# A Strassen output projection in a hybrid encoder block: loads asked for in another order, rows split in halves, stores and row sums placed later

## The chip, the cores and the metric

The kernel runs on one core of one Trainium2 chip. The metric is device time in microseconds (us) of one execution; a version's figure is the median of its runs. The trace counts from the span's start.

## The reference

One encoder block, sequence 1024, width 1024. All operands are float32. A short gated convolution mixer (`ya`) and a bidirectional gated DeltaNet (`yb`) are projected, gated, merged, projected again, added to the input and normalised:

```python
ya = a_cg * dwconv_centred(a_bg * a_x, conv_a_w[l])
ya = ya * jax.nn.silu(a_z)
ya = ya @ w_pa[l]
...
yb = (o * jax.nn.silu(z)).reshape(bsz, slen, VAL_DIM).astype(dt_)
yb = yb @ w_pb[l]
merged = jax.nn.sigmoid(gate_a_raw) * ya + jax.nn.sigmoid(gate_b_raw) * yb
x = x + gate[:, None, :] * (merged @ w_o[l])
return rmsnorm(x, final_norm_w)
```

## The kernel before

Every float32 product is made of three one-pass matmuls: each operand is split into `hi` (a rounded copy, made by ScalarE, ACT) and `lo` (the rest, `raw - hi`, made by VectorE, DVE, or by GpSimd, POOL), and hi·hi, lo·hi and hi·lo are added in PSUM. So before TensorE (PE) can use a row or a weight, three things have come one after another: a load, an ACT copy and a subtraction.

The order of the program, late stages first in importance here:

- **Up to about 765 us**: projections and the DeltaNet, ordered by a scheduler in the code (`Scheduler`).
- **The pairs, 765 to 1109 us** (the loop over `steps`, L1549): column blocks two at a time by Strassen's method, seven products of 12 matmuls each per pair instead of eight. Groups are `bg`, `ax`, `cg`, `az` for four pairs, then gates `gb`. After each `az`, the mixer's output rows `y` are stored (`y_d`), and `y_sum` (L1439) makes the sums `T1`, `T3`, `T2`, `T4` of their quarters, which the next stage's Strassen products take as operands; they are stored to `t_d`. A list `late` holds such DVE jobs; each step of the loop pops one.
- **Gate blocks 6 and 7** (`gate_block`, L1480), plain products, 1109 to 1131 us.
- **Stage pa, the output projection `ya @ w_pa`** (the loop over `pa_steps`, L1598), 28 steps, four Strassen pairs of seven products, 1131 to 1227 us. Its operands are 28 half-row tiles `yop` (`B11`, `B21`, `B22` from `y_d`; `T1` to `T4` from `t_d`), loaded by `fetch_operand` and split by `split` (L1545: ACT, then DVE). The first pair's products are A11, A12, S4, S2, S1, S3, then, after one product of the second pair, A22. S1 needs `T1`, S3 `T3`, A22 `T4`. S3 and A22 add into the PSUM bank of S2, so they also wait until the earlier content has been copied out to `u_pa`. Weights come through `Pair.load` (four raw tiles `wr_pa` per pair), `prep` (the sums `S_pa` on DVE and the hi copy on ACT) and `rest` (the lo part on DVE).
- **Stage pb, `yb @ w_pb` and the merge** (L1645), eight blocks `j` of 48 matmuls, 1227 to 1322 us. Its rows `yb` are fetched by `fetch_b` into the slots of `yop` tiles that pa has finished with, then split into `bhi`, `blo`. Its weights `wpb[j]` go through `wtile`: two raw tiles `wraw` (two buffers, which the rows of `w_o`, `wor`, use as well), ACT for `wh_pb`, POOL for `wl_pb`. Each product is multiplied by `sgb`, added to the loaded row `mr` and split again (`mhi`, `mlo`).
- **The final projection `merged @ w_o`** and the norm, to the end.

From the pairs to the end of pa, DVE, ACT, POOL and SP each run in the order in which the code is written (`manual_schedule`); from pb on, a scheduler in the compiler orders them, and `tc.high_priority()` lets it hoist. PE runs its list in order. All loads and stores of these stages are issued by SyncE (SP), one queue: an entry that waits holds up all behind it. Line numbers in the profile are those of this kernel; L323 is a helper that records every operation of the earlier stages.

Of the kernel before, what the change touches and what calls it, by code (L numbers as in the profile page):

```python
# [9 lines left out]
F32 = mybir.dt.float32  # L10
# [6 lines left out]
P = 128  # L17
# [311 lines left out]
def block(ctx: ExitStack, tc: tile.TileContext, x, c, wada, wadag, badaT, nwT, win, wab, cva, cvq,  # L329
          alog, dtb, gnw, wpa, wpb, wo, fnw, out, dbg=None):  # L330
# [37 lines left out]
    def ch(c, w=P):  # L368
        return slice(w * c, w * c + w)
# [875 lines left out]
    def bank(pl, name):  # L1245
        return pl.tile([P, 512], F32, tag="b", name=name)

    def wtile(src, name):
        hi = wp.tile([P, KT * P], F32R, tag="whi", name=f"wh_{name}")
        lo = wp.tile([P, KT * P], F32R, tag="wlo", name=f"wl_{name}")  # L1250
        for q in range(2):
            raw = wp.tile([P, 512], F32, tag="wraw", name=f"wr_{name}_{q}")
            Q.dma_start(raw, src[:, ch(q, 512)])
            S.activation(hi[:, ch(q, 512)], raw, AF.Copy)  # L1254
            G.tensor_tensor(lo[:, ch(q, 512)], raw, hi[:, ch(q, 512)].bitcast(F32), ALU.subtract)  # L1255
        return hi, lo
# [138 lines left out]
    def mixed(name, j0, place):  # L1395
        seen = [0, 0]

        def full(n, b):
            if (n, b) not in outs:
                outs[n, b] = btile("out", f"{n}{j0 + b}", 4, (P, T))  # L1400
            return outs[n, b]

        def consume(b, half, ps, add):
            sl = ch(half, 512)
            x = xpads[b][:, 2 + 512 * half : 514 + 512 * half]
            seen[b] += 1
# [24 lines left out]
            if seen[b] == 2:
                Q.dma_start(y_d[j0 + b], a)
            if sum(seen) == 4:
                late.extend(partial(y_sum, j0 // 2, i, *[outs.pop((n, b)) for n in ("a", "c") for b in range(2)])
                            for i in range(1))

        return Pair(name, j0, consume, place)

    def y_sum(m, i, a0, a1, c0, c1):  # L1439

        r11, r12, r21, r22 = (t[:, ch(h, 512)] for t in (a0, a1) for h in range(2))
        t1, t3, t2, t4 = (t[:, ch(h, 512)] for t in (c0, c1) for h in range(2))
        V.tensor_tensor(*((t1, r12, r11), (t3, r22, r12), (t2, r22, t1), (t4, r21, t2))[i], ALU.subtract)
        if i % 2:
            Q.dma_start(t_d[m, i // 2], (c0, c1)[i // 2])
        if i < 3:
            late.insert(0, partial(y_sum, m, i + 1, a0, a1, c0, c1))

    def conv3(acc, b, j, i):
        x, c = xpads[b][:, 1 + i : 1 + i + T], cva_t[:, j, i : i + 1]  # L1450
# [40 lines left out]
        steps.pop(0)  # L1491
        pairs[0].after(n, early[n])
    yop = {n: [None] * 4 for n in hop}
    pas = []

    def merged_pair(j0, place):
        gates = []

        def load_gates():
            for b in range(2):  # L1500
                gates.append(btile("out", f"sga{j0 + b}", 4, (P, T)))
                Q.dma_start(gates[b], sga_d[j0 + b])

        seen = [0, 0]

        def consume(b, half, ps, add):
            g = gates[b][:, ch(half, 512)]
            if add is not None:
                t = btile("tmp", f"t_pa{j0}{b}{half}", 2)
                V.tensor_tensor(t, ps, add, ALU.add)  # L1510
# [79 lines left out]
    def fetch_b(k):  # L1590
        for i, l in enumerate((bhi, blo)):
            p, kk = places[2 * k + i]
            l.append(hp.tile([P, T], F32R, tag=f"h{p}{kk}", name=f"b{('hi', 'lo')[i]}{k}", bufs=1))
        Q.dma_start(blo[k].bitcast(F32), yb_d[k])

    todo = [(n, m) for n in ("T1", "T3", "T4") for m in range(4)]
    fetched = {"S3": (2, 3), "S1": (4, 5), "A22": (6, 7)}
    for i, (p, n) in enumerate(pa_steps):  # L1598
        look_ahead(pa_steps, i + AHEAD + 5)
        advance(pa_steps, i + AHEAD)  # L1600
        for _ in range(2):
# [6 lines left out]
        if i == len(pa_steps) - 10:
            for k in range(2):
                fetch_b(k)  # L1610
        if p is pas[-1] and n in fetched:
            for k in fetched[n]:
                fetch_b(k)
        if i >= len(pa_steps) - 6:
            for k in ((0,), (1,), (2, 3), (4,), (5, 6), (7,))[i - len(pa_steps) + 6]:
                split(bhi[k], blo[k])
# [25 lines left out]
    with tc.tile_pool(name="ms", bufs=2, reuse_waits="tile", side="right") as ms:  # L1642
        sc_t = ms.tile([P, T], F32, tag="sc", name="sc_g", bufs=1)
        Q.dma_start(sc_t, sc_d.to_broadcast([P, T]))
        for j in range(8):  # L1645
            with tc.high_priority():
                w = wtile(wpb[j], f"pb{j}")
            m = ms.tile([P, T], F32, tag="m", name=f"mr{j}")
            Q.dma_start(m, m_d[j])
            sg = ms.tile([P, T], F32, tag="sg", name=f"sgb{j}")  # L1650
            Q.dma_start(sg, sgb_d[j])
            wt = ms.tile([P, T], F32, tag="wadag", name=f"wadag{j}")
            Q.dma_start(wt, wadag[j])
            for half in range(2):
                ps = product(w, bhi, blo, half, f"pb{j}")
                sl = ch(half, 512)
                V.tensor_tensor(sg[:, sl], ps, sg[:, sl], ALU.mult)
                G.tensor_tensor(m[:, sl], m[:, sl], sg[:, sl], ALU.add)
# [124 lines left out]
```

## Time and profile before

| | |
|---|---|
| median of 3 runs | 1420.57 us (1417.34 to 1420.83) |
| profiled execution | 1419.85 us |
| its span in the trace | 1418.1 us |
| PE busy in the span | 1362.4 us (96%) |
| DVE, ACT, POOL busy | 919.1, 632.4, 462.8 us |
| mean granted clock of PE | 0.989 |

PE is busy nearly always, so what can be saved is the time in which it stands still or runs at a lower granted clock. A busy share of 100% in a slice says nothing about the rate; the column PEclk does (1.00 is the full clock). "Idle before" an instruction is time in which its engine did nothing, and the arrow names what ended it.

### The profile page before, as it was taken

How to read it: one execution, taken by the hardware profiler on the slowest of the kernel's cores; microseconds unless marked ns; L12 is line 12 of the kernel's file. 1: busy time of each engine (PE TensorE's matmuls, PEld its weight loads, DVE VectorE, ACT ScalarE, POOL GpSimd, SP SyncE). 2: the span in 40 equal slices, each digit the busy share in tenths (PEclk: the TensorE clock that was granted, in tenths of full speed). 3: DMA queues.
4: the chain of work that ended last, by engine and by line, in shares of the span. 5: the costliest groups of instructions: out<-in, count | busy, mean ns of one | idle time of the engine just before them, and what ended most of it. 6: DMA issues, size and time to landing. Idle time of an engine off the chain costs nothing.

```text
span 1418.1 us, 22459 instructions
## 1 busy us (share of the span) xinstructions
PE 1362.4 (96%) x8450; PEld 1135.1 (80%) x8450; DVE 919.1 (65%) x1583; ACT 632.4 (45%) x1535; POOL 462.8 (33%) x702
## 2 busy tenths in 40 slices
PE   5899999999999999999999999999999969899998
PEld 5678888887889888888887878788787848688886
DVE  6868175657667676856766877777676556763335
ACT  5447575664648384745444232223223532423211
POOL 2004837574738474756410000000000100266301
PEclk9999999999999999999999999999999989999999
DMA  9315341515141323323123121121312854586402
GB/s 355 97 60 153 112 92 66 150 38 142 31 119 61 98 82 89 92 60 91 54 97 134 60 99 64 75 89 51 125 49 90 296 178 163 197 302 198 178 15 104
DMA packets 128334, 163.31 MB, mean 115 GB/s; under 512 B 75105, under 2 KB 75489, under 8 KB 128226
## 3 DMA queue, kind: packets, MB, share of 16 engines
q1 hardware_dynamic: 127794, 160.58, 34.9%
q8 instruction: 66, 1.08, 0.3%
q10 hardware_dynamic: 432, 1.31, 0.3%
q14 instruction: 42, 0.34, 0.1%
HBM read 128.16 MB, written 33.69 MB: 114 GB/s over the span
## 4 chain that ended last, share of the span: by engine, by line
PE 85%; DVE 8%; DMA 3%; ACT 2%; issue 2%; POOL 0%; SPq 0%; POOLq 0%; ACTq 0%; DVEq 0%
PE pp_ga L215 6%; PE pp_z L215 6%; PE pp_q L215 6%; PE cb L215 6%; PE pp_v L215 6%; PE pp_k L215 5%; PE ps_cg_S L1348 4%; PE o L215 4%; PE ps_ax_S L1348 4%; PE ps_pa_S L1348 3%; PE ps_az_S L1348 2%; PE pp_pb L1264 2%; PE ps_bg_S L1348 2%; PE fo L1688 2%; PE fo L1687 2%; PE fo L1689 2%
## 5 line engine op out<-in xcount | busy, mean ns | idle before, releaser
L323 POOL TENSOR_TENSOR E<-E,et 128x30 f32<-128x30 f32 (+7 forms) x240 | 122.5, 510 | 16.8
L1255 POOL TENSOR_TENSOR wl_gb<-wr_gb,wh_gb 128x512 fp32r<-128x512 f32 x4 | 5.1, 1294 | 351.5 <-ACT wh_gb L1254 351.5
L323 POOL TENSOR_TENSOR et<-E 128x30 f32<-128x30 f32 (+7 forms) x240 | 109.2, 455 | 30.0 <-DMA E<-s 13.4
L323 DVE SCALAR_TENSOR_TENSOR S<-S,exps,cb 128x128 f32<-128x128 f32 x96 | 29.6, 344 | 59.3 <-PE cb L215 58.5
L1255 POOL TENSOR_TENSOR wl_pb<-wr_pb,wh_pb 128x512 fp32r<-128x512 f32 x16 | 25.1, 1577 | 128.1 <-DMA blo<-yb_d 104.7
L323 ACT ACTIVATE vw<-cb,cols 128x128 f32<-128x128 f32 x112 | 36.3, 364 | 68.1 <-PE cb L215 67.7
L1264 PE MATMUL pp_pb<-blo,wh_pb 128*128 128x512 f32 x128 | 51.5, 402 | 4.2 <-DVE blo L1547 4.2
L215 PE MATMUL pp_z<-hhi,wh_z 128*128 128x512 f32 x128 | 52.8, 412 | 0.0
L215 PE MATMUL pp_z<-hhi,wl_z 128*128 128x512 f32 x128 | 52.7, 412 | 0.0
L215 PE MATMUL pp_z<-hlo,wh_z 128*128 128x512 f32 x128 | 52.7, 412 | 0.0
L215 PE MATMUL pp_ga<-hhi,wl_ga 128*128 128x512 f32 x128 | 51.7, 404 | 0.0
L215 PE MATMUL pp_ga<-hhi,wh_ga 128*128 128x512 f32 x128 | 51.6, 403 | 0.0
L215 PE MATMUL pp_ga<-hlo,wh_ga 128*128 128x512 f32 x128 | 51.5, 402 | 0.0
L323 DVE SCALAR_TENSOR_TENSOR r<-cb,negeg,vp 128x128 f32<-128x128 f32 x112 | 34.5, 345 | 25.4 <-PE cb L215 24.9
L1263 PE MATMUL pp_pb<-bhi,wh_pb 128*128 128x512 f32 x128 | 50.7, 396 | 0.0
L1265 PE MATMUL pp_pb<-bhi,wl_pb 128*128 128x512 f32 x128 | 50.4, 393 | 0.0
L323 ACT ACT_TABLE_LOAD x38 | 48.8, 1283 | 1.5 <-PEq L1778 0.8
L323 DVE SCALAR_TENSOR_TENSOR vT<-xpad,cvq_t,vT 128x1024 f32<-128x1024 f32 x32 | 48.7, 1523 | 0.3
L215 PE MATMUL pp_q<-hhi,wl_q 128*128 128x512 f32 x112 | 44.7, 399 | 2.4 <-issue 2.4
L323 ACT ACTIVATE vn<-cb,cols 128x128 f32<-128x128 f32 x128 | 41.4, 372 | 10.4 <-PE cb L215 10.4
L215 PE MATMUL pp_q<-hhi,wh_q 128*128 128x512 f32 x112 | 45.6, 407 | 0.0
L215 PE MATMUL pp_v<-hhi,wl_v 128*128 128x512 f32 x112 | 45.4, 406 | 0.0
(951 smaller groups left out, 4422.0 us busy)
## 6 DMA issues: line engine op xcount, KB each, us to landing
wada<-in_wada SPq DMA_DIRECT2D x16, 512.0 KB, 8.5
D<-gr_d SPq DMA_DIRECT2D x16, 512.0 KB, 7.1
wr_bg<-in_win SPq DMA_DIRECT2D x18, 256.0 KB, 3.0
xt<-in_x SPq DMA_DIRECT2D x8, 512.0 KB, 8.9
wr_k<-in_win SPq DMA_DIRECT2D x16, 256.0 KB, 2.8
wr_q<-in_win SPq DMA_DIRECT2D x16, 256.0 KB, 2.8
wr_v<-in_win SPq DMA_DIRECT2D x16, 256.0 KB, 3.0
wr_ga<-in_win SPq DMA_DIRECT2D x16, 256.0 KB, 2.9
```

What stands on the lines that cost most here:

```text
L215: getattr(self.pe, what)(out, *ins, **kw)
L323: self._sched.record(self._name, lambda: real(*args, **kw), outs, ins, cost, extra, table, op == "memset", port)
L1255: G.tensor_tensor(lo[:, ch(q, 512)], raw, hi[:, ch(q, 512)].bitcast(F32), ALU.subtract)
L1263: PE.matmul(ps, wh, mhi[k][:, sl], start=i == 0, stop=False)
L1264: PE.matmul(ps, wh, mlo[k][:, sl], start=False, stop=False)
L1265: PE.matmul(ps, wl, mhi[k][:, sl], start=False, stop=i == KT - 1)
L1348: PE.matmul(ps, w, r, start=first and m == i == 0, stop=m == 3 and i == 2, skip_group_check=True)
L1687: PE.matmul(ps, mhi[k][:, ch(t)], wh, start=k == 0, stop=False)
L1688: PE.matmul(ps, mlo[k][:, ch(t)], wh, start=False, stop=False)
L1689: PE.matmul(ps, mhi[k][:, ch(t)], wl, start=False, stop=k == KT - 1)
```

## The change

- **Row sums.** After an `az` pair (the last one excepted), four empty entries go into `late` ahead of the four `y_sum` jobs, so they run four steps later, and on SP their two stores come behind the next four weight loads.
- **Second pair's weights.** `look_ahead(pa_steps, 6)` after gate block 6, so its `wr_pa` loads stand ahead of the loads of `T1`, `T3`, `T4` instead of behind them. The second pair's gate rows `sga`, till now loaded there, are loaded after step 1.
- **Splits of `T1`, `T3`, `T4`** start at step 1 of pa, not 0: two tiles per step.
- **Stores of pa** (`m_d`) are not asked for where the row is complete, but after the next step's product.
- **Rows for pb** are loaded and split in halves of 512 columns; rows 0 and 1 after step 14 (before: 18), split at steps 16 and 17 (before: 22 and 23). Rows 2 to 7 have their first halves split first, the second halves at the last two steps.
- **First weights of pb** are asked for by the code after step 19 and split after step 26, where before the compiler's scheduler had hoisted both (loads at 1112 us).

The diff, without the passing of arguments:

```diff
-                late.extend(partial(y_sum, j0 // 2, i, *[outs.pop((n, b)) for n in ("a", "c") for b in range(2)])
-                            for i in range(1))
+                rows = [outs.pop((n, b)) for n in ("a", "c") for b in range(2)]
+                late.extend([None] * (4 if j0 < 6 else 0) + [partial(y_sum, j0 // 2, i, *rows) for i in range(4)])
...
-                Q.dma_start(m_d[j0 + b], gates[b])
+                stores.append((m_d[j0 + b], gates[b]))
...
-    look_ahead(pa_steps, 7)
-    pas[1].extra()
+    look_ahead(pa_steps, 6)
...
-        Q.dma_start(blo[k].bitcast(F32), yb_d[k])
+        for h in range(2):
+            Q.dma_start(blo[k][:, ch(h, 512)].bitcast(F32), yb_d[k][:, ch(h, 512)])
...
+    last = len(pa_steps)
+    fetched = {last - 14: (0, 1), last - 6: (2, 3), last - 5: (4, 5), last - 4: (6, 7)}
+    split_at = {last - 12: ((0, 0), (0, 1)), last - 11: ((1, 0), (1, 1)), last - 5: ((2, 0), (3, 0)),
+                last - 4: ((4, 0), (5, 0)), last - 3: ((6, 0), (7, 0)), last - 2: ((2, 1), (3, 1)),
+                last - 1: ((4, 1), (5, 1), (6, 1), (7, 1))}
...
-        for _ in range(2):
+        for _ in range(2 * (i > 0)):
...
+        waiting, stores[:] = stores[:], []
         p.product(n)
+        for k in fetched.get(i, ()):
+            fetch_b(k)
+        for dst, src in waiting:
+            Q.dma_start(dst, src)
+        if i in (1, 8, 15):
             pas[i // 7 + 1].extra()
...
+        if i == last - 9:
+            raws = wraws(wpb[0], "pb0")
+        if i == last - 2:
+            w_next = wtile(wpb[0], "pb0", raws)
+        for k, h in split_at.get(i, ()):
+            split(bhi[k][:, ch(h, 512)], blo[k][:, ch(h, 512)])
...
-                w = wtile(wpb[j], f"pb{j}")
+                w = wtile(wpb[j], f"pb{j}") if j else w_next
```

PE's order is the same in both kernels, instruction by instruction. Three places on the other engines follow.

SP, from gate block 6's store (`xpad_119`) to the first load of `T1` (`yop_T_0`), before:

```order
L1485 DMA sgb_d<-xpad_119 128x1024
L1502 DMA sga_10880<-sga_d 128x1024
L1502 DMA sga_10882<-sga_d 128x1024
L1485 DMA sgb_d<-xpad_120 128x1024
L1543 DMA yop_T_0_10976<-t_d 128x512
```

and now:

```order
L1488 DMA sgb_d<-xpad_119 128x1024
L1324 DMA wr_pa_10880<-in_wpa 128x512
L1324 DMA wr_pa_10882<-in_wpa 128x512
L1324 DMA wr_pa_10884<-in_wpa 128x512
L1324 DMA wr_pa_10886<-in_wpa 128x512
L1488 DMA sgb_d<-xpad_120 128x1024
L1546 DMA yop_T_0_10980<-t_d 128x512
```

The second pair's four weight loads stand where the two `sga` loads stood, 1 MB each way; before, they followed all twelve loads of `T1`, `T3` and `T4`.

DVE at the first splits of `T1` (the first `S_pa` rows here are the second pair's weight sums), before:

```order
L1547 TENSOR_TENSOR yop_T_0_10976<-yop_T_0_10976 128x512
L1547 TENSOR_TENSOR yop_T_1_10978<-yop_T_1_10978 128x512
L1310 TENSOR_TENSOR S_pa_11031<-wr_pa_11000,wr_pa_11002 128x512
L1310 TENSOR_TENSOR S_pa_11033<-S_pa_11031,wr_pa_11004 128x512
L1333 TENSOR_TENSOR wloS_pa_10920<-S_pa_11008,whiS_pa_10919 128x512
L1547 TENSOR_TENSOR yop_T_2_10980<-yop_T_2_10980 128x512
L1547 TENSOR_TENSOR yop_T_3_10982<-yop_T_3_10982 128x512
```

and now:

```order
L1315 TENSOR_TENSOR S_pa_11023<-wr_pa_10880,wr_pa_10882 128x512
L1315 TENSOR_TENSOR S_pa_11025<-S_pa_11023,wr_pa_10884 128x512
L1338 TENSOR_TENSOR wloS_pa_10924<-S_pa_11004,whiS_pa_10923 128x512
L1550 TENSOR_TENSOR yop_T_0_10980<-yop_T_0_10980 128x512
L1550 TENSOR_TENSOR yop_T_1_10982<-yop_T_1_10982 128x512
L1513 TENSOR_TENSOR t_pa_11048<-ps_pa_A_11035,e_pa_11021 128x512
L1515 TENSOR_TENSOR sga_10807<-t_pa_11048,sga_10807 128x512
L1338 TENSOR_TENSOR wlS_pa_11028<-S_pa_11025,whS_pa_11027 128x512
L1550 TENSOR_TENSOR yop_T_2_10984<-yop_T_2_10984 128x512
L1550 TENSOR_TENSOR yop_T_3_10986<-yop_T_3_10986 128x512
```

The weight sums now stand ahead of all splits of `T1`, and three other pieces (a PSUM read `t_pa`, its product with `sga`, a weight's lo part) stand between the two halves of `T1`.

ACT in stage pb at block 2's weights (`wh_pb` of `wr_pb_0`, `wr_pb_1`) and block 0's merged rows (`mhi`), before:

```order
L1637 ACTIVATE woh_11824<-wor_1_11822 128x512
L1254 ACTIVATE wh_pb_11828<-wr_pb_0_11830 128x512
L1254 ACTIVATE wh_pb_11828<-wr_pb_1_11834 128x512
L1659 ACTIVATE mhi_11642<-mr_11676 128x512 x2
L1659 ACTIVATE mhi_11643<-mr_11757 128x512
```

and now:

```order
L1649 ACTIVATE woh_11848<-wor_1_11846 128x512
L1259 ACTIVATE wh_pb_11856<-wr_pb_0_11852 128x512
L1671 ACTIVATE mhi_11676<-mr_11700 128x512 x2
L1259 ACTIVATE wh_pb_11856<-wr_pb_1_11853 128x512
L1671 ACTIVATE mhi_11677<-mr_11781 128x512
```

The second half of block 2's weights now stands behind block 0's two merged rows.

More of the change, by code (lines that the diff above doesn't have):

```diff
@@ L1246, in bank, with wraws, wtile @@
         return pl.tile([P, 512], F32, tag="b", name=name)
-    def wtile(src, name):
+    def wraws(src, name):
+        raws = [wp.tile([P, 512], F32, tag="wraw", name=f"wr_{name}_{q}") for q in range(2)]
+        for q, raw in enumerate(raws):
+            Q.dma_start(raw, src[:, ch(q, 512)])
+        return raws
+    def wtile(src, name, raws=None):
+        raws = raws or wraws(src, name)
         hi = wp.tile([P, KT * P], F32R, tag="whi", name=f"wh_{name}")
         lo = wp.tile([P, KT * P], F32R, tag="wlo", name=f"wl_{name}")
-        for q in range(2):
-            raw = wp.tile([P, 512], F32, tag="wraw", name=f"wr_{name}_{q}")
-            Q.dma_start(raw, src[:, ch(q, 512)])
+        for q, raw in enumerate(raws):
             S.activation(hi[:, ch(q, 512)], raw, AF.Copy)
@@ L1445, in y_sum @@
             Q.dma_start(t_d[m, i // 2], (c0, c1)[i // 2])
-        if i < 3:
-            late.insert(0, partial(y_sum, m, i + 1, a0, a1, c0, c1))
     def conv3(acc, b, j, i):
@@ L1493, in block @@
     yop = {n: [None] * 4 for n in hop}
-    pas = []
+    stores = []
     def merged_pair(j0, place):
@@ L1556, in block @@
             p.product(n)
-        if late:
-            late.pop(0)()
+        job = late.pop(0) if late else None
+        if job:
+            job()
         if i + 4 == len(steps):
@@ L1593, in fetch_b @@
             l.append(hp.tile([P, T], F32R, tag=f"h{p}{kk}", name=f"b{('hi', 'lo')[i]}{k}", bufs=1))
-        Q.dma_start(blo[k].bitcast(F32), yb_d[k])
+        for h in range(2):
+            Q.dma_start(blo[k][:, ch(h, 512)].bitcast(F32), yb_d[k][:, ch(h, 512)])
     todo = [(n, m) for n in ("T1", "T3", "T4") for m in range(4)]
-    fetched = {"S3": (2, 3), "S1": (4, 5), "A22": (6, 7)}
+    last = len(pa_steps)
[3 more added lines that the diff above has]
+                last - 1: ((4, 1), (5, 1), (6, 1), (7, 1))}
     for i, (p, n) in enumerate(pa_steps):
@@ L1604, in block @@
                 split(*yop[n4][m])
+        waiting, stores[:] = stores[:], []
         p.product(n)
-        if i in (8, 15):
-            pas[i // 7 + 1].extra()
[L1608 to L1616, printed above, removed]
+        for k in fetched.get(i, ()):
[3 more added lines that the diff above has]
+        if i in (1, 8, 15):
+            pas[i // 7 + 1].extra()
+        if i == last - 9:
[4 more added lines that the diff above has]
+            split(bhi[k][:, ch(h, 512)], blo[k][:, ch(h, 512)])
+    for dst, src in stores:
+        Q.dma_start(dst, src)
     sctx.close()
```

## Prediction

> **What bounds the kernel now.** First the page's busy line: PE is at 96%, so I ask where the other 4% lie, and where PE is busy but slow. The waits of PE, asked for the pairs (690 to 1100 us) and then for stages pa and pb (1080 to 1270 us), give nearly all of it:
>
> ```profile
> PE 1362.4 (96%) x8450; PEld 1135.1 (80%) x8450; DVE 919.1 (65%) x1583; ACT 632.4 (45%) x1535; POOL 462.8 (33%) x702
> ...
> PE ps_bg_S L1348 <- DVE u_bg L1356: 2.5, 4, 0.7
> ...
> PE ps_pa_S L1348 <- ACT yop_T L1546: 8.3, 1, 8.3
> PE ps_pa_S L1348 <- DVE u_pa L1356: 4.7, 1, 4.7
> PE pp_pb L1264 <- DVE blo L1547: 4.2, 3, 3.6
> PE ps_pa_S L1348 <- ACT u_pa L1354: 0.9, 1, 0.9
> ```
>
> The last four add to 18.1 us. The windows show what follows a long wait (second figure PE busy, sixth the granted clock):
>
> ```profile
> 1150.00:1155.00 5.00, 3.23 (x6) 1.77 (x6) 4.29 (x8) 4.46 (x9) 0.00 (x0) 0.50 0.10 37
> 1155.00:1160.00 5.00, 4.14 (x18) 3.40 (x19) 4.90 (x9) 2.37 (x5) 0.00 (x0) 0.98 0.15 52
> 1165.00:1170.00 5.00, 3.58 (x9) 2.83 (x10) 3.86 (x7) 0.91 (x2) 0.00 (x0) 0.55 0.00 2
> ```
>
> After the 8.3 and the 4.7 us waits PE runs at half clock for some microseconds. So I measure each place by PE's own progress. The timeline of PE, where S1 and the second pair's S1 start, then where block 0, 1 and 2 of pb start:
>
> ```profile
> 1141.92 0.63 PE L1348 MATMUL ps_pa_S<-yop_T,whiS_pa 128*128 128x512 f32 x2
> 1174.74 0.63 PE L1348 MATMUL ps_pa_S<-yop_T,whiA_pa 128*128 128x512 f32 x2
> 1227.07 0.40 PE L1263 MATMUL pp_pb<-bhi,wh_pb 128*128 128x512 f32 x1
> 1244.73 0.39 PE L1263 MATMUL pp_pb<-bhi,wh_pb 128*128 128x512 f32 x1
> 1255.72 0.39 PE L1263 MATMUL pp_pb<-bhi,wh_pb 128*128 128x512 f32 x1
> ```
>
> Block 1 takes 10.99 us for 48 matmuls, 0.229 each; block 0 took 17.66, so 6.7 us are lost there. Between the first two rows lie five products, 60 matmuls, 13.7 us at that rate; they took 32.8, so 19.1 us are lost there.
>
> Why S1 waited is read from ACT, DVE and SP:
>
> ```profile
> 1139.33 1.30 ACT L1546 ACTIVATE yop_T<-yop_T 128x512 fp32r<-128x512 f32 x2 [5.12 <-DMA yop_T<-t_d]
> 1150.54 0.63 ACT L1326 ACTIVATE whS_pa<-S_pa 128x512 fp32r<-128x512 f32 x1 [9.42 <-DVE S_pa L1310]
> 1139.99 1.36 DVE L1547 TENSOR_TENSOR yop_T<-yop_T 128x512 fp32r<-128x512 f32 x2 [5.85 <-ACT yop_T L1546]
> 1149.02 0.69 DVE L1310 TENSOR_TENSOR S_pa<-wr_pa,wr_pa 128x512 f32<-128x512 f32 x1 [7.67 <-DMA wr_pa<-in_wpa]
> 1124.88 0.74 SPq L1485 DMA_DIRECT2D sgb_d<-xpad  x1
> 1133.65 0.32 SPq L1485 DMA_DIRECT2D sgb_d<-xpad  x1
> 1134.03 8.19 SPq L1543 DMA_DIRECT2D yop_T<-t_d  x12
> 1142.98 14.16 SPq L1319 DMA_DIRECT2D wr_pa<-in_wpa  x8
> ```
>
> T1's first tiles land at 1139.3 and are split. The other two have to stand behind the second pair's weight sum, whose weights were asked for at 1142.98, behind all twelve T loads, and landed at 1149. It is not the rows that PE waited for, but ACT and DVE held up, in order, by weights that no one needed yet.
>
> **Part 1, the weights and splits in pa.** The four weight loads take the place of two `sga` loads, as many bytes, after gate block 6's store (1124.88). Bytes move at
>
> ```profile
> 1120.00:1125.00 5.00, 5.00 (x24) 4.09 (x23) 4.41 (x8) 4.92 (x10) 0.00 (x0) 1.00 1.05 390
> ```
>
> 390 GB/s, 0.67 us per 256 KB. The store landed, by the DMA view,
>
> ```profile
> sgb_d<-xpad SPq DMA_DIRECT2D x1, 512.0 KB, 7.9
> ```
>
> 7.9 us after its issue, at 1132.8; four loads of 0.67 us behind it are in by 1135.5, 4 us ahead of T1. So the weight sums and `whS_pa` are done before T1 comes, and the waits of 7.67 and 9.42 us go. The T loads themselves still follow gate block 7's store (1133.65), so they are asked for no sooner. They may land up to 1.3 us sooner, as 0.5 MB of pb's weights leave the stream ahead of them; or at 1139.3 as now.
>
> What is late next is DVE: from T1's first lo part to T4's last, its order now has 27 pieces, the 12 splits and 15 others. Its rate when it has all it needs, first row and the row after the last of 19 pieces:
>
> ```profile
> 1151.72 1.29 DVE L1547 TENSOR_TENSOR yop_T<-yop_T 128x512 fp32r<-128x512 f32 x2 [0.67 <-ACT yop_T L1546]
> 1164.38 1.29 DVE L1547 TENSOR_TENSOR yop_T<-yop_T 128x512 fp32r<-128x512 f32 x2 [0.70 <-ACT yop_T L1546]
> ```
>
> 12.66 us less the 0.70 of waiting is 0.63 a piece; that wait (sum, hi copy, then the split) stays, now before T4. From 1140.0, piece 22 (`u_pa`, which frees the bank for A22) ends at 1140.0 + 22 x 0.63 + 0.7 = 1154.6. PE, unheld, would be there at 1141.9 + 3 x 2.75 = 1150.2, so it stands 4.4 us in all up to A22's start: 2.5 in S3 (T3's third tile is piece 14, done at 1148.8, needed at 1144.7 + 1.6 = 1146.3), the rest ahead of A22. T4's third tile is piece 26, done at 1157.1, needed at 1154.6 + 1.6 = 1156.2: 0.9 more. A22 ends at 1154.6 + 2.75 + 0.9 = 1158.2; before, it ended at 1174.74 - 2.75 = 1172.0. Gain 13.8, or 15.0 with T1 1.2 us sooner. I take 14.2, nearer to the unchanged landing, since its request is unmoved. `sga` for the second pair, now behind the T loads, lands by about 1149 (the weights there did); its first use is in the pair's third product, after 1160.
>
> Does the clock stay up? The 0.9 us wait left 0.98, a 3.65 us one halved it (pb's, below); mine are up to 2.5 us. If they halved it, two dips of 1.7 us would make the gain 10.8. The Trainium skill (TensorE: Matmul & The Clock Gate, What's actually happening) says that half clock comes after an idle window of about 3.4 us; by that the dips cost nothing and the gain stays 14.2.
>
> **Part 2, rows for pb.** Why block 0 stalled: DVE is full and `blo` last.
>
> ```profile
> 1237.09 0.78 PE L1264 MATMUL pp_pb<-blo,wh_pb 128*128 128x512 f32 x1 [3.65 <-DVE blo L1547]
> 1225.00:1230.00 5.00, 5.00 (x23) 4.11 (x22) 4.90 (x7) 1.94 (x3) 1.80 (x1) 1.00 0.26 107
> 1234.75 2.28 DVE L1547 TENSOR_TENSOR blo<-blo,bhi 128x1024 fp32r<-128x1024 f32 x1
> 1190.00:1200.00 10.00, 10.00 (x45) 8.23 (x44) 6.03 (x11) 2.17 (x4) 0.00 (x0) 1.00 0.76 262
> L1547 DVE TENSOR_TENSOR blo<-blo,bhi x8: 1211/1224/2303, 1215.1 to 1234.8; 128x1024 fp32r<-128x1024 f32 x8
> ```
>
> The last lo part ended at 1237.0. Halves cost 16 x 0.61 instead of 8 x 1.22: the same. But two rows' four halves go to steps 16 and 17 (2.4 us, where DVE has 4 of 10 us free), and six second halves (3.7 us) behind what product half 0 needs. So row 7's first half is ready at 1237.0 - 2.4 - 3.7 = 1230.9 at the latest, against a need at 1227.07 + 7 x 0.69 = 1231.9. The second halves are needed from 1235 on, and DVE has them by about 1235. I take the whole 6.7 us back; its lower bound is 4.2 (the waits gone, the clock not).
>
> The weights of block 0 are the price: till now made by POOL at 1216.85, they now come after step 26 in the code, when DVE is full. The last pair's A11 ends at 1227.07 - 2 x 2.75 = 1221.6; ACT then has `e_pa`, two half rows and the weights' first half, 4 x 0.6, so POOL starts at 1224.0 at the earliest.
>
> ```profile
> 1216.85 4.58 POOL L1255 TENSOR_TENSOR wl_pb<-wr_pb,wh_pb 128x512 fp32r<-128x512 f32 x2 [104.70 <-DMA blo<-yb_d]
> 1233.01 1.27 POOL L1255 TENSOR_TENSOR wl_pb<-wr_pb,wh_pb 128x512 fp32r<-128x512 f32 x1 [3.41 <-DVE t_pa L1510]
> ```
>
> At 2.29 each (beside DVE) they are done at 1226.3 and 1228.6, needed at 1227.5 and 1230.3: just in time. At 1.27 (alone) there is more room. The Trainium skill (GPSIMD Engine Reference, Key points) says that GpSimd shares its SBUF interface with VectorE and contends with two-input work there; by that this move goes into the worst place, and 2.29, as the trace shows it, is the right price.
>
> Later blocks' weights go through two `wraw` buffers that start their rounds 7 us later than now. Block 2's second half also stands behind block 0's merge on ACT. That merge took
>
> ```profile
> 1247.62 1.29 DVE L1657 TENSOR_TENSOR sgb<-pp_pb,sgb 128x512 f32<-128x512 f32 x2 [10.59 <-DMA sgb<-sgb_d]
> 1248.39 3.54 POOL L1658 TENSOR_TENSOR mr<-mr,sgb 128x512 f32<-128x512 f32 x2 [0.38 <-DVE sgb L1657]
> ```
>
> and 0.63 on ACT, from `sgb`'s landing to 1252.6: 5 us. A tile's round takes 2.7 (landing, least) + 0.63 + 1.3 to 2.3 (POOL; rows under (c)), so block 1's two tiles, one after the other from 1228.6, are done at 1238 to 1240; behind that stands `sgb` on SP, with 2.0 us of other bytes ahead and 4.1 to landing: 1244 to 1246. Then 5.0 + 0.63 + 1.3 to 2.3: the weights are ready at 1251 to 1254, needed at 1227.07 + 22.0 + 3.2 = 1252.3. The wait is 0 to 1.7 us; I take 1.0.
>
> **Part 3, row sums.** Three of the four 0.7 us waits are the boundaries at which `y_sum` stands ahead of S_bg on DVE:
>
> ```profile
> 842.31 0.50 PE L1348 MATMUL ps_bg_S<-sums_D,whS_bg 128*128 128x512 f32 x1 [0.70 <-DVE u_bg L1356]
> 840.41 0.63 ACT L1326 ACTIVATE whiS_bg<-S_bg 128x512 fp32r<-128x512 f32 x1 [3.58 <-DVE S_bg L1310]
> ```
>
> Two pieces of 0.6 go from before S_bg, so its copy, then `e_bg`, then `u_bg` come 1.2 us sooner; the 0.70 goes. Three times: 2.1 us. The pieces come back where DVE has idle time. Bounds 0 and 2.1. The stores moved past four weight loads, and the `m_d` stores moved by a step, hold nothing that PE needs soon: 0, covered by SP's idle time; if the cover fails, a step, 2.75 us.
>
> **Sum.** 14.2 + 6.7 + 2.1 - 1.0 = 22.0 us. The profiled execution took 1419.85 us (span 1418.1), 0.7 under the median; so 1397.9 on its scale, 1398.6 on the median's.
>
> **Rivals.**
> (a) PE's short waits in pa pull the clock down, or T1 and DVE are a little later: gain 10.8 in part 1, time 1402. For it: nothing shows a wait of 1 to 3 us in this stage; against: 0.9 left the clock alone.
> (b) POOL beside a full DVE holds block 0's weights: 2 to 4 us of the 6.7 come back, time 1401 to 1403. For: 1.2 us of room; against: weights are read one column block at a time.
> (c) Pb's feed gives part back. A raw tile's round is landing, ACT, POOL:
>
> ```profile
> L1255 POOL TENSOR_TENSOR wl_pb<-wr_pb,wh_pb x14: 1269/1300/2292, 1227.8 to 1303.5; 128x512 fp32r<-128x512 f32 x14
> DMA to landing us min/median/max: 2.7/4.1/5.9
> ...
> 1246.00:1330.00 84.00, 84.00 (x377) 69.28 (x376) 41.68 (x52) 21.99 (x36) 53.77 (x38) 1.00 0.69 234
> ```
>
> Median 4.1 + 0.63 + 1.3 = 6.0, at three tiles in two buffers 9.0 us a block, under 10.99. With every maximum 8.8, 13.2 a block: 2.2 x 7 blocks = 15.5 given back, time 1414.
> (d) Slower: the same feed, with the new place of the merge on ACT adding 1.1 us and more to every round, 9.9: 14.9 a block, 3.9 x 7 = 27 us, time 1398.6 + 27 = 1426. It turns the sign from a block of 14.1 us on (22 / 7 more than 11). Against: PE was busy in all 84 us of the last row, and the merge stands so before some blocks' weights, not all.
> (e) The change does not do what it says: the weights land late all the same, ACT holds T1 as now, gain under 4: 1417.
>
> **How the numbers follow.** Forecast (1395 to 1401) 0.62; (a) 0.13; (b) 0.08; more than forecast, DVE quicker or T1 sooner (1390 to 1395) 0.05; (c), to 1414, 0.05; (e) 0.04; (d) 0.03. A measurement here tells 0.3% (4.3 us) from no change. Faster: all but (d) and (e): 0.93; same 0.04; slower 0.03. The range 1393.5 to 1406 takes in both bounds of part 1, (a), (b) and the start of (c).
>
> **What would show it.** Right: PE's wait on ACT `yop_T` gone, the second pair's `S_pa` before 1137, A22 ending near 1158, small waits on `yop_T` or `u_pa` of 4 to 6 us in sum, no half-clock window in pa; block 0 of pb in 11 us; three waits on `u_bg` gone. Wrong: a wait of several us on `wl_pb` or `wh_pb` in blocks 0 to 3, `sga` or `wr_pa` as releasers in pairs two to four, or T1 landing after 1141.

## The result and the profile after

| | before | after |
|---|---|---|
| median | 1420.7 us (1417.34 to 1420.88) | 1402.47 us (1398.71 to 1405.76) |
| profiled execution, span | 1419.85, 1418.1 us | 1401.2, 1399.5 us |
| mean granted clock | 0.989 | 0.994 |

The ratio is 0.9876, 95% interval 0.9846 to 0.9907: 18.2 us faster, against 22.0 forecast. In a later session the same two kernels gave 1400.71 and 1418.05 us, 0.9881 (0.9861 to 0.9900).

First the page's busy line, then two answers on the waits of PE, for the pairs (690 to 1100 us) and for the stages from 1080 us on:

```profile
PE 1357.9 (97%) x8450; PEld 1132.6 (81%) x8450; DVE 918.7 (66%) x1591; ACT 633.0 (45%) x1543; POOL 461.9 (33%) x702
```

```profile
PE ps_gb_S L1353 <- DVE u_gb L1361: 1.4, 1, 1.4
...
PE ps_bg_S L1353 <- DVE u_bg L1361: 0.4, 1, 0.4
```

```profile
PE pp_pb L1269 <- DVE blo L1550: 1.8, 1, 1.8
PE pp_pb L1270 <- POOL wl_pb L1260: 1.7, 2, 1.1
PE ps_pa_S L1353 <- ACT yop_T L1549: 1.6, 1, 1.6
PE ps_pa_S L1353 <- DVE yop_T L1550: 1.3, 2, 0.7
```

Of the four waits on `u_bg`, 2.5 us in sum, one of 0.4 is left. In pa the 8.3 and 4.7 us are gone and 2.9 us stand in their place. In pb the 4.2 us on `blo` became 1.8, but 1.7 us on POOL's `wl_pb` are new. PE's progress in pa, where S1 and the second pair's S1 start:

```profile
1139.27 0.63 PE L1353 MATMUL ps_pa_S<-yop_T,whiS_pa 128*128 128x512 f32 x2
...
1156.83 0.63 PE L1353 MATMUL ps_pa_S<-yop_T,whiA_pa 128*128 128x512 f32 x2
```

17.56 us, where it took 32.82. For pb I count from one block's first weight load (PEld) to the next one's (block 7 to the first of the products behind it), since a matmul's own start shifts when the clock changes inside a block:

```profile
1208.99 0.19 PEld L1268 LDWEIGHTS pp_pb<-bhi,wh_pb 128*128 128x128 f32 x1
1223.91 0.33 PEld L1268 LDWEIGHTS pp_pb<-bhi,wh_pb 128*128 128x128 f32 x1
1304.68 0.19 PEld L1699 LDWEIGHTS fo<-woh,mhi 128*128 128x128 f32 x1
```

Block 0 took 14.92 us (17.66 before). The last row is the start of the final projection. Cut at such marks, the two spans differ like this:

| stretch of PE | before | after | gain |
|---|---|---|---|
| pairs to gate blocks | 350.65 | 347.66 | 2.99 |
| S1 to the second pair's S1 | 32.82 | 17.56 | 15.26 |
| block 0 of pb to the final projection | 96.46 | 95.69 | 0.77 |
| block 0 alone | 17.66 | 14.92 | 2.74 |

The rest of pa (52.33 and 52.38) and the end (94.8 in both) are alike. So the two parts in the pairs and in pa gave nearly all; part 2, forecast at 6.7 less 1.0, gave 0.8 us. The windows (second figure PE busy, sixth the clock) show why a 1.8 us wait cost more than itself:

```profile
1145.00:1150.00 5.00, 3.65 (x16) 2.62 (x14) 4.27 (x7) 2.98 (x6) 0.00 (x0) 1.00 0.69 265
1150.00:1155.00 5.00, 4.05 (x17) 3.03 (x17) 4.59 (x9) 0.77 (x2) 0.00 (x0) 1.00 0.00 0
...
1220.00:1225.00 5.00, 4.49 (x13) 3.59 (x14) 2.26 (x4) 1.26 (x2) 2.46 (x2) 0.68 0.85 259
```

The waits in pa leave the clock at 1.00; behind the one in pb eight matmuls run at half clock. And this is what DVE and POOL did before it, from the timeline of each:

```profile
1208.16 0.69 DVE L1515 TENSOR_TENSOR sga<-t_pa,sga 128x512 f32<-128x512 f32 x1
...
1209.49 1.42 DVE L1515 TENSOR_TENSOR sga<-t_pa,sga 128x512 f32<-128x512 f32 x1
1210.83 1.79 DVE L1373 TENSOR_TENSOR u_pa<-u_pa,e_pa 128x512 f32<-128x512 f32 x1
...
1217.71 1.07 DVE L1515 TENSOR_TENSOR sga<-t_pa,sga 128x512 f32<-128x512 f32 x1
1218.71 3.55 DVE L1550 TENSOR_TENSOR blo<-blo,bhi 128x512 fp32r<-128x512 f32 x4
```

```profile
1209.07 3.00 POOL L1260 TENSOR_TENSOR wl_pb<-wr_pb,wh_pb 128x512 fp32r<-128x512 f32 x2 [99.10 <-ACT wh_pb L1259]
1216.42 1.81 POOL L1260 TENSOR_TENSOR wl_pb<-wr_pb,wh_pb 128x512 fp32r<-128x512 f32 x1 [4.35 <-ACT wh_pb L1259]
1218.19 1.71 POOL L1650 TENSOR_TENSOR wol<-wor,woh 128x512 fp32r<-128x512 f32 x1
```

The same piece, `sga`, takes 0.69 us at 1208.16 and 1.42 at 1209.49, when POOL is at work. Over the stretch DVE's pieces of this kind take 3.3 us more than at 0.61 to 0.69 each. That is my first theory for block 0; its rival is that DVE was simply full and the second halves too late whatever POOL did.

### The profile page after: what moved, and what is told of

Same layout as the page of the kernel before. It is cut to its first block, busy times and chain, and to the rows that moved or that the text cites. A ratio compares the mean times of both kernels' runs of the same rounds, so it can differ in the third digit from the quotient of the medians.

```text
span 1399.5 us, 22490 instructions
## 1 busy us (share of the span) xinstructions
PE 1357.9 (97%) x8450; PEld 1132.6 (81%) x8450; DVE 918.7 (66%) x1591; ACT 633.0 (45%) x1543; POOL 461.9 (33%) x702
## 3 DMA queue, kind: packets, MB, share of 16 engines
q10 hardware_dynamic: 432, 1.31, 0.3%
## 4 chain that ended last, share of the span: by engine, by line
PE 88%; DVE 5%; DMA 2%; issue 2%; ACT 1%; POOL 1%; SPq 1%; POOLq 0%; DVEq 0%; ACTq 0%
PE pp_ga L215 6%; PE pp_z L215 6%; PE cb L215 6%; PE pp_q L215 5%; PE pp_v L215 5%; PE pp_k L215 5%; PE ps_cg_S L1353 4%; PE o L215 4%; PE ps_ax_S L1353 4%; PE ps_az_S L1353 4%; PE ps_bg_S L1353 3%; PE ps_pa_S L1353 3%; PE fo L1699 2%; PE fo L1700 2%; PE fo L1701 2%
## 5 line engine op out<-in xcount | busy, mean ns | idle before, releaser
L323 POOL TENSOR_TENSOR E<-E,et 128x30 f32<-128x30 f32 (+7 forms) x240 | 117.5, 490 | 16.9
L323 DVE SCALAR_TENSOR_TENSOR qT<-xpad,cvq_t,qT 128x1024 f32<-128x1024 f32 x32 | 45.7, 1427 | 0.3
```

What stands on the lines that cost most here:

```text
L323: self._sched.record(self._name, lambda: real(*args, **kw), outs, ins, cost, extra, table, op == "memset", port)
```

## Experiments

All times are medians, with the ratio to the kernel before, run beside it. "Block 0" and "S1 to S1" are the two stretches above, from each run's trace.

**u_weights: part 1's order undone** (in the changed kernel).

```diff
-    look_ahead(pa_steps, 6)
+    look_ahead(pa_steps, 7)
+    pas[1].extra()
...
-        for _ in range(2 * (i > 0)):
+        for _ in range(2):
...
-        if i in (1, 8, 15):
+        if i in (8, 15):
```

> The changed kernel (1402.5 us) with the weights of pa's second pair, its gate rows and the start of the T splits as in the kernel before. Theory 1 (the waits of pa came from the order of these loads and splits on SP, ACT and DVE): S1 of the first pair waits 8 us on ACT yop_T again, the second pair's S_pa is released by wr_pa near 1147, a half-clock window follows, S1 to second S1 takes 31 to 33 us instead of 17.6, time 1416 to 1418. Rival 1 (part 1's gain came from pb's first weights having left the stream ahead of T1, so that T1 lands sooner): S1 to second S1 stays within 3 us of 17.6, time 1402 to 1406.

1413.78 us, 0.9975 (0.9963 to 0.9987). Its waits of PE from 1080 us on, and the row of ACT that ends the long one:

```profile
PE ps_pa_S L1353 <- ACT yop_T L1549: 8.0, 1, 8.0
PE ps_pa_S L1353 <- DVE u_pa L1361: 3.0, 1, 3.0
```

```profile
1149.84 0.63 ACT L1331 ACTIVATE whS_pa<-S_pa 128x512 fp32r<-128x512 f32 x1 [10.57 <-DVE S_pa L1315]
```

ACT stands 10.57 us before a copy that no product needs yet, and S1 to S1 is 31.43 us: theory 1, and the rival falls. This order is worth 31.43 - 17.56 = 13.9 us. The time came out under the 1416 expected, though its profiled span, 1415.4, is 15.9 above the changed kernel's. The edit undoes three things together (the weights' loads, the gate rows', the start of the splits), and their shares are not parted. Up to the pairs all these kernels have the same code, and yet their profiled executions got there between 755.5 and 761.5 us. Medians of a few runs carry that scatter, so I read the causes from the stretches, but each is from one execution, and they do not all repeat alike. Pairs to gate blocks repeats within 0.1 us. S1 to S1 took 17.5 to 17.6 us in seven executions of the changed kernel and of edits that do not touch it, but 18.0 to 18.1 in three others (u_sums, w_early, pool_twice), which ran beside u_weights; against those the order is worth 13.4. Block 0 took 14.92 and, in a second execution of the changed kernel (after_again, below), 13.93.

**u_sums: the row sums not put off.**

```diff
-                late.extend([None] * (4 if j0 < 6 else 0) + [partial(y_sum, j0 // 2, i, *rows) for i in range(4)])
+                late.extend([partial(y_sum, j0 // 2, i, *rows) for i in range(4)])
```

> The changed kernel with the row sums as soon as in the kernel before (no empty entries ahead of them). Theory 1: the three waits of 0.7 us on DVE u_bg at the pair boundaries come back, gate blocks start 2.1 to 3.0 us later than in the changed kernel's profile (1106.0), time 1404.5 to 1405.5. Rival (the three waits went for another reason, the shared queue's order for instance, or other work in the pairs takes up the slack): no wait on u_bg comes back, gate blocks within 0.5 us of 1106.0, time 1402.5.

1403.92 us, 0.9906 (0.9891 to 0.9921). Pairs to gate blocks: 350.66 us, against 347.66, and the waits on `u_bg` are back (PE's waits, 690 to 1100 us):

```profile
PE ps_bg_S L1353 <- DVE u_bg L1361: 2.6, 4, 0.7
```

Theory 1: 3.0 us. The time is 0.6 us under the range expected, and the median alone would not have told the cause.

**u_pb: part 2 undone.** Rows whole, fetched after step 18 and split from step 22 on; the two lines for `raws` and `w_next` gone, so that the compiler places block 0's weights.

```diff
-    fetched = {last - 14: (0, 1), last - 6: (2, 3), last - 5: (4, 5), last - 4: (6, 7)}
+    fetched = {last - 10: (0, 1), last - 6: (2, 3), last - 5: (4, 5), last - 4: (6, 7)}
...
-                w = wtile(wpb[j], f"pb{j}") if j else w_next
+                w = wtile(wpb[j], f"pb{j}")
```

> The changed kernel with all of part 2 undone: rows for pb whole and fetched and split where the kernel before did, pb's first weights left to the compiler's scheduler again. Theory 1 (part 2 gains 2.7 us in block 0 and gives about 1.9 back in blocks 1 and 3): block 0 takes 17.0 to 17.9 us with a wait of about 3.6 us on blo and a slow clock, block 3 falls back to 11.0, and T1 lands up to 1 us later; time 1403 to 1404.5. Rival (part 2 as priced in the prediction, 5.7 us net, or the first weights gave back more than the rows gained): 1408, or under 1402.

1403.48 us, 0.9900 (0.9884 to 0.9917). PE's waits from 1080 us on:

```profile
PE pp_pb L1269 <- DVE blo L1550: 4.1, 3, 3.5
PE ps_pa_S L1353 <- DVE yop_T L1550: 2.2, 2, 1.5
```

Block 0 18.54 us (0.6 over the range), blocks 1 to 7 at 10.98 or 10.99, block 0 to final projection 97.36: part 2 is worth 1.7 us there. S1 to S1 is 18.40, 0.8 more, and 18.52 in the next run, the other one in which block 0's weights are loaded ahead of `T1` again. So a little of what part 1 gained probably came from part 2's edit, though 0.5 of such a difference can be scatter.

**u_first: only block 0's weights left to the compiler**, rows in halves.

> The changed kernel with only pb's first weights as before (asked for and made where the compiler's scheduler puts them, ahead of the splits of rows 4 and 5); rows stay in halves. Theory 1 (POOL beside a full DVE is what block 0 lost; pieces made earlier find DVE with gaps, but the next block's weights move up into the same place): wl_pb's wait of 0.6 goes, blo's waits fall to 0.6 to 1.5 us in sum, no half clock, block 0 takes 12 to 14 us. Rival (DVE alone is too slow for the halves): block 0 keeps its 1.8 us wait on blo and takes 14.3 to 15 us. Time by theory 1 1399.5 to 1402, if the later blocks keep their pace; by the rival 1402 to 1403.

1407.26 us, 0.9921 (0.9904 to 0.9939). Block 0 fell to 12.94 us with two waits on `blo` of 0.6 and 0.7, as theory 1 said; but blocks 2 and 4 took 15.13 and 15.96, and block 0 to final projection 100.89, 5.2 more than in the changed kernel:

```profile
PE pp_pb L1270 <- POOL wl_pb L1260: 4.2, 2, 2.4
...
PE pp_pb L1269 <- DVE blo L1550: 1.4, 2, 0.7
PE pp_pb L1268 <- ACT wh_pb L1259: 1.0, 1, 1.0
```

**w_early: block 0's weights made after step 22.**

```diff
-        if i == last - 2:
+        if i == last - 6:
             w_next = wtile(wpb[0], "pb0", raws)
```

> The changed kernel with pb's first weights (wh_pb, wl_pb) made after step 22 instead of step 26, so that POOL works where DVE still has idle time, before the second halves of the rows are subtracted. Theory 1 (block 0 of pb lost 4 us to POOL's late weight and to DVE pieces that ran at half speed beside POOL): wl_pb and blo waits and the slow clock of block 0 go, block 0 takes 11.0 to 11.8 us instead of 14.9, time 1398 to 1399.5. Rival (DVE is full and the second halves late whatever POOL does): only the 0.62 us wait on wl_pb goes, the 1.8 us wait on blo and the half clock stay, block 0 takes 14 to 14.5 us, time 1401.5 to 1402.5.

1404.80 us, 0.9909 (0.9893 to 0.9926): both theories had it as fast as the changed kernel or faster, and its median is higher. The intervals overlap, but block 0 to final projection is 102.94 us, 7.2 longer. Block 0 took 13.90, without a slow clock, which is no less than the changed kernel's 13.93 without one; blocks 2, 3 and 4 took 13.35, 12.26 and 17.56, with these waits of PE:

```profile
PE pp_pb L1270 <- POOL wl_pb L1260: 4.8, 3, 2.1
PE pp_pb L1269 <- DVE blo L1550: 2.0, 3, 0.7
...
PE pp_pb L1268 <- ACT wh_pb L1259: 1.4, 1, 1.4
```

Both runs tell the same: with block 0's weights out of the way, block 1's weights move up, so that one of their POOL pieces and one of a row of `w_o` stand beside DVE's last four splits (4.67 us in both runs), and the later blocks' weights come late. That they come late because of the shared raw tiles would be rival (c) of the prediction, which I had given 0.05; these two runs do not show the reason.

**pool_twice: more work for POOL, none for DVE.** The result of the two pieces is not used.

```diff
             w_next = wtile(wpb[0], "pb0", raws)
+            for q in range(2):
+                hq = w_next[0][:, ch(q, 512)].bitcast(F32)
+                G.tensor_tensor(btile("raw", f"twice{q}", 8), hq, hq, ALU.subtract)
```

> The changed kernel with two more POOL subtractions of the same size right behind pb's first weights, whose result nothing reads: added work on POOL alone, beside DVE's last splits of the rows. Theory 1 (POOL slows DVE's two-input pieces there): DVE's sga and blo pieces near 1211 to 1222 take 1.0 to 1.8 us instead of 0.6 to 0.7 in more places, the wait on blo in block 0 grows from 1.8 to about 3 to 4 us, block 0 takes 16 to 18 us, time 1404 to 1406. Rival (the lateness of the weights alone matters, DVE is not slowed by POOL): block 0 stays at 14.9 within 0.5, time 1402.5.

1402.46 us, 0.9896 (0.9881 to 0.9911). Block 0 took 17.92 us and `blo`'s waits 3.5 us in sum, as theory 1 said. The last four splits:

```profile
1219.52 4.65 DVE L1550 TENSOR_TENSOR blo<-blo,bhi 128x512 fp32r<-128x512 f32 x4
```

```profile
1219.01 1.72 POOL L1653 TENSOR_TENSOR wol<-wor,woh 128x512 fp32r<-128x512 f32 x1 [1.89 <-issue]
1220.68 1.73 POOL L1260 TENSOR_TENSOR wl_pb<-wr_pb,wh_pb 128x512 fp32r<-128x512 f32 x1
```

4.65 us for four pieces, 3.55 in the changed kernel, 2.49 where POOL rests (below): about 1.1 for each POOL piece beside them. Block 3 took 10.99 instead of 12.33, so block 0 to final projection is only 2.3 us longer, which the expectation of 1404 had left out; that the median did not rise even by that is within the scatter of the medians.

**lo_dve: block 0's lo parts on DVE instead**, at the same step: DVE does more, POOL less.

```diff
-            G.tensor_tensor(lo[:, ch(q, 512)], raw, hi[:, ch(q, 512)].bitcast(F32), ALU.subtract)
+            eng.tensor_tensor(lo[:, ch(q, 512)], raw, hi[:, ch(q, 512)].bitcast(F32), ALU.subtract)
...
-            w_next = wtile(wpb[0], "pb0", raws)
+            w_next = wtile(wpb[0], "pb0", raws, V)
```

> The changed kernel with the lo part of pb's first weights made by DVE instead of POOL, at the same step: DVE has two pieces more (1.2 us), POOL two fewer. Theory 1 (each POOL piece beside DVE costs DVE 0.7 to 1.1 us): the sga and u_pa pieces near 1210 take 0.69 instead of 1.42 and 1.79, DVE ends its last blo 0.3 to 0.8 us sooner although it does more, blo's wait falls to 1.0 to 1.5 us, wl_pb's wait goes, block 0 takes 12 to 14 us, time 1399.5 to 1401.5. Rival (DVE is simply full, POOL does not slow it): the last blo ends 1.2 us later, blo's wait grows to 3.0 us, block 0 takes 16 to 17 us, time 1404.

1401.09 us, 0.9883 (0.9866 to 0.9900). DVE's timeline:

```profile
1206.07 0.69 DVE L1515 TENSOR_TENSOR sga<-t_pa,sga 128x512 f32<-128x512 f32 x1
1206.68 0.68 DVE L1373 TENSOR_TENSOR u_pa<-u_pa,e_pa 128x512 f32<-128x512 f32 x1
...
1210.54 1.28 DVE L1260 TENSOR_TENSOR wl_pb<-wr_pb,wh_pb 128x512 fp32r<-128x512 f32 x2
...
1214.27 4.67 DVE L1550 TENSOR_TENSOR blo<-blo,bhi 128x512 fp32r<-128x512 f32 x4
```

`sga` and `u_pa` take 0.69 and 0.68, and the last `blo` ends 12.8 us after block 0's start instead of 13.3, with two pieces more. The rival falls. The forecast for block 0 fell too, 17.98 us instead of 12 to 14: DVE's order puts `wl_pb` at 1210.54, and PE waits for it,

```profile
PE pp_pb L1270 <- DVE wl_pb L1260: 4.3, 1, 4.3
```

behind which the clock is halved. The place in the order was wrong, not the engine. The time, inside the range, hid that miss, since blocks 1 to 7 ran at 10.98 to 11.23.

**lo_dve_early: both edits**, step 22 and DVE.

> As the run before, and pb's first weights made after step 22, where DVE still waits for rows. Theory 1: DVE makes the two pieces in its idle time, POOL has nothing there until block 1's weights, so what is left is 1.0 to 3.1 us from those and from the w_o rows: blo's waits 0 to 1.5 us in sum, no half clock, block 0 takes 11 to 13 us, time 1398.5 to 1400.5 if blocks 2 to 4 keep the changed kernel's pace, about 1403 if they lose 4 to 6 us to late weights as they did when POOL made them early. Rival (the second halves are late whatever POOL does): block 0 stays above 14 us, time 1402.

1397.40 us, 0.9856 (0.9839 to 0.9872), 3.3 and 5.1 under the changed kernel's two medians, from other sessions; the intervals of the ratios overlap, and block 0 to final projection is 2.1 us shorter (93.62). Block 0 took 14.04 us, more than expected: two waits on `blo`, 1.6 us in sum, and half clock behind them; block 1 11.75. Blocks 2 to 7 took 10.98 or 10.99 each, where block 3 of the changed kernel took 12.33 and 13.79.

**lo_dve_two: block 1's lo parts on DVE as well; lo_dve_two_wo: each `w_o` row one block later too; after_again: the changed kernel beside them.**

```diff
-                w = wtile(wpb[j], f"pb{j}") if j else w_next
+                w = wtile(wpb[j], f"pb{j}", None, V if j == 1 else G) if j else w_next
...
-            load_wo(0, j)
+            for k in ((), (0,), (1,), (2,), (3,), (4,), (5,), (6, 7))[j]:
+                load_wo(0, k)
```

> The changed kernel unaltered, beside the next two on the same chip. Both theories: 1402.5 us, within 3; block 0 of pb 14.9 us with a 1.8 us wait on blo and eight matmuls at half clock behind it.

> Weights of block 0 made early by DVE as in the last run, and block 1's lo parts by DVE too. Theory 1 (each POOL piece beside DVE's last splits costs DVE up to 1.1 us; a DVE piece costs 0.6): two POOL pieces at 1211 and 1216 go, DVE has 1.2 us more, only the w_o row's piece is left on POOL; blo's waits fall from 1.6 us in sum to 0 to 1.0, the half clock goes, block 0 takes 11 to 12.5 us, time 1395.5 to 1397.5. Rival (DVE full): blo's waits grow by 1.2 us to about 2.8, block 0 takes 15 us, time 1398.5.

> As the one before, and the loading of each w_o row put off by one block, so that POOL has nothing to do while DVE splits the last rows. Theory 1: all of DVE's pieces between 1204 and 1220 take 0.6 to 0.7 us, no wait on blo, no half clock, block 0 takes 11.0 to 11.3 us, block 1 11.0, time 1394 to 1396 if the later blocks keep their pace. Rival (DVE full, whoever works beside it): a wait on blo of over 1 us stays and block 0 takes over 13 us.

lo_dve_two: 1402.18 us, 0.9891 (0.9875 to 0.9908). lo_dve_two_wo: 1400.09, 0.9872 (0.9857 to 0.9886). Block 0 took 13.89 and 12.05 us; `blo`'s waits in sum were 1.5 and 0.8. In the second, every piece of DVE from 1204 to 1220 took its usual time, 0.68 or 0.69 where it stands alone. POOL was not idle all that time, though: a `w_o` piece stands beside the last four splits, and here it was POOL that took longer.

```profile
1217.83 2.49 DVE L1550 TENSOR_TENSOR blo<-blo,bhi 128x512 fp32r<-128x512 f32 x4
```

```profile
1217.74 3.73 POOL L1650 TENSOR_TENSOR wol<-wor,woh 128x512 fp32r<-128x512 f32 x1 [107.72 <-ACT woh L1649]
```

3.73 us is 2.5 more than the 1.27 of a POOL piece alone. So which engine pays is not settled by their being busy together; why it was POOL here, and DVE in the other runs, is open. And with DVE at its full rate block 0 still missed its forecast (11.0 to 11.3): a wait of 0.8 us on `blo` stayed, so DVE's own load, with the two pieces added, counts too. In the first, block 0 (forecast 11 to 12.5) and `blo`'s sum (0 to 1.0) missed their ranges as well, beside the one `w_o` piece that was left, with half clock behind. Block 3 took 13.44 and 15.66: block 0's gain was given back on the weights, so the times were missed. In after_again, block 3 took 13.79 as well, and block 0 13.93: the same wait, in PE's timeline,

```profile
1221.26 0.50 PE L1269 MATMUL pp_pb<-blo,wh_pb 128*128 128x512 f32 x1 [1.80 <-DVE blo L1550]
```

and no slow clock behind it:

```profile
1220.00:1225.00 5.00, 3.74 (x16) 3.09 (x17) 3.01 (x4) 1.26 (x2) 2.40 (x3) 1.00 0.78 249
```

**lo_dve_two_own: the `w_o` rows get two raw tiles of their own**, on top of lo_dve_two.

```diff
-            raw = wp.tile([P, 512], F32, tag="wraw", name=f"wor{n}_{k}")
+            pl, tag = (wp, "wraw") if n else (ms, "wor")
+            raw = pl.tile([P, 512], F32, tag=tag, name=f"wor{n}_{k}")
```

> As the kernel with block 0's and block 1's lo parts on DVE, and the rows of w_o get two raw tiles of their own instead of sharing wraw with pb's weights. Theory 1 (what blocks 2 to 4 lose comes from three raw tiles a block going through two buffers): block 2's weights are in before block 1 starts, no wait on wl_pb or wh_pb in blocks 1 to 4, each 11.0 us; POOL has only block 2's lo parts beside DVE's last splits, blo's wait 0 to 1.0 us, block 0 takes 11 to 12.5 us; time 1393.5 to 1396. Rival (the order of ACT and POOL behind the merge is what is late, not the buffers): waits of 1 to 2.5 us on pb's weights stay in blocks 2 to 4, time 1398 to 1402.

1396.28 us, 0.9840 (0.9816 to 0.9863): the fastest of all, though over the 1393.5 to 1396 expected. Block 0 took 11.65 us, blocks 1 to 7 10.98 or 10.99, block 0 to final projection 90.45 where the changed kernel took 95.69 and 95.72. DVE's last splits, POOL's first piece beside pb and PE's wait:

```profile
1217.80 2.49 DVE L1550 TENSOR_TENSOR blo<-blo,bhi 128x512 fp32r<-128x512 f32 x4
```

```profile
1221.95 2.55 POOL L1260 TENSOR_TENSOR wl_pb<-wr_pb,wh_pb 128x512 fp32r<-128x512 f32 x2 [111.59 <-ACT wh_pb L1259]
```

```profile
PE pp_pb L1269 <- DVE blo L1550: 0.4, 1, 0.4
```

What held up blocks 2 to 4 of lo_dve_two went with the sharing of `wraw`. Sharing alone does not make the wait: lo_dve_early and u_pb share the two buffers as well, and their blocks 2 to 7 took 10.98 or 10.99. Whether the buffers themselves count, or the order on SP that follows from them (the `w_o` rows now stand behind the weights), this run does not part.

## Why the prediction was right, and where it was not

**The sign, the range and the main mechanism held.** 14.2 of the 22.0 us were to come from the order of weights and splits, and u_weights shows it. The median, 1402.47, is outside the narrower 1395 to 1401 that had most of the chance, and the total is nearer to 22.0 than its parts deserve: parts 1 and 3 came out 1.1 and 0.9 us over their terms, part 2 4.9 under, so that misses made up for one another in part.

**Part 1, 14.2 forecast, 15.26 measured.** Its bounds were 13.8 and 15.0. The weights' order gives 13.4 to 13.9 (u_weights), the earlier `T1` up to 0.8 (u_pb), a rest of 0.5 or more was not parted. `T1` came sooner than the upper bound had it: 4.3 us from the first request on SP to the copy on ACT, where it was 5.3, and the request itself, which I had as unmoved, came 24.3 us after the start of the gate blocks, where it was 25.4. Gate block 7's store ahead of it went out sooner, too. In PE's progress that is 2.1 us, against the 1.2 of the bound.

```profile
1130.28 7.02 SPq L1546 DMA_DIRECT2D yop_T<-t_d  x12
```

```profile
1134.60 1.32 ACT L1549 ACTIVATE yop_T<-yop_T 128x512 fp32r<-128x512 f32 x2 [2.23 <-DMA yop_T<-t_d]
```

DVE had the second pair's sums out of the way by then, and its 27 pieces, which were to take 17.7 us, took 18.1:

```profile
1129.81 0.69 DVE L1315 TENSOR_TENSOR S_pa<-wr_pa,wr_pa 128x512 f32<-128x512 f32 x1
...
1135.27 1.38 DVE L1550 TENSOR_TENSOR yop_T<-yop_T 128x512 fp32r<-128x512 f32 x2 [3.44 <-ACT yop_T L1549]
...
1152.07 1.28 DVE L1550 TENSOR_TENSOR yop_T<-yop_T 128x512 fp32r<-128x512 f32 x2
```

PE's waits in pa were 2.9 us in sum, not 4 to 6. Rival (a) did not come: no slow clock there in any of the twelve executions that have this order.

**Part 3, 2.1 forecast, 2.99 measured.** The three waits went; the term was mis-sized, because a wait costs PE more than its idle time. The changed kernel's timeline of PE in block 0:

```profile
1218.31 0.40 PE L1268 MATMUL pp_pb<-bhi,wh_pb 128*128 128x512 f32 x1
1220.51 0.51 PE L1269 MATMUL pp_pb<-blo,wh_pb 128*128 128x512 f32 x1 [1.80 <-DVE blo L1550]
1220.85 0.40 PE L1270 MATMUL pp_pb<-bhi,wl_pb 128*128 128x512 f32 x1
```

Two steps take 2.54 us where two of 0.229 would do: 2.08 lost for 1.80 idle. Of the 0.28 more, 0.17 lies in how idle time is counted (a row is 0.40 long, though the next matmul starts after 0.229), and 0.11 in the first step after the wait (0.34). 0.28 for each of three waits is 0.84; the waits themselves were 2.14 (0.70, 0.72 and 0.72), and 2.14 + 0.84 = 2.98.

**Part 2, 6.7 less 1.0 forecast, 0.8 measured: the step that failed** is "Halves cost 16 x 0.61 instead of 8 x 1.22: the same ... The second halves are needed from 1235 on, and DVE has them by about 1235". DVE's rate of 0.61 did not hold there beside POOL. I priced POOL beside DVE (2.29) and left DVE beside POOL at its price alone, although the forecast itself moved POOL's weights into that stretch, and a quoted row showed it: a `blo` of 2.28 us where the median is 1.22. Beside POOL, DVE lost 3.3 us; hence the 1.80 us wait, and in the profiled execution a stretch of half clock that cost 1.6 us, 0.6 of them in block 1. The run lo_dve_two_wo bears that out: without the loss, and with two pieces (1.2 us) more, DVE's last split ends 11.4 us after block 0's start instead of 13.3; that is 1.9 us sooner, and 3.3 - 1.2 is 2.1. That POOL's weights are late themselves was rival (b), 0.57 to 0.62 us of wait. The Trainium skill (SBUF — State Buffer, SBUF: two separate sides) says that the pair of ports which DVE and GpSimd share is an exclusive lock, held for a whole instruction by whichever starts first, where DVE has two SBUF inputs. The rows fit with it: 1.27 (POOL alone) + 0.61 is 1.9, and `u_pa` beside POOL took 1.79, while in lo_dve_two_wo POOL was the one held up.

**The later weights, 1.0 forecast** at block 2: the wait came at block 3 and was 1.06 us, 2.52 in after_again. As rival (c) had it, such a wait went when the `w_o` rows left the two buffers that pb's weights use (lo_dve_two_own, against lo_dve_two). Why that rival's 9.0 us a block, under the 10.99 of PE, did not keep the wait away was not tried.

## What to carry to other kernels

Before moving work into a full stretch of DVE, list what POOL does beside it: here a subtraction moved from POOL to DVE, 0.6 us, cost DVE less than POOL's doing it next to DVE, up to 1.1 us (in one run POOL waited and DVE lost nothing), provided that it stands in a gap of DVE's order and not behind what PE waits for. A weight that nobody needs yet, ahead in an in-order queue, can cost more than the data that PE waits for; look at what stands before the late piece, not only at the piece. When a cure moves the loss to later blocks, look for what they share, here two raw tiles.

## What the runs showed of the hardware

**The clock does not follow from a wait's length.** One wait of 1.80 us halved the clock in one execution of the changed kernel and not in another. One of 1.31 us did (lo_dve_two, with one of 0.2 two microseconds ahead), and so did two of 0.92 and 0.72 (lo_dve_early); one of 2.09 us did not (w_early), and 1.6 with 0.7 us soon behind it, in pa, never did in twelve executions. The Trainium skill (TensorE: Matmul & The Clock Gate, What's actually happening) speaks of a free-running window of about 3.4 us: that the same wait has both outcomes fits with it, but that the clock falls only after an idle window is contradicted by the 1.31 us wait, far shorter than a window. What decides stays open.

**A wait costs PE about 0.28 us beyond the idle time that the trace counts**, as worked out above.
